# A two-layer hybrid encoder on one core: a hand-written planner with new instruction costs, two buffers for the recurrence's keys and decays, and a key move without a chain

## The chip, the cores and the metric

The kernel runs on one core of a Trainium2 chip. The metric is the device time of one execution in microseconds (us); it was 1365.31 us as the median of three runs (1364.5 to 1365.95). One more execution was profiled; the trace below is of that one.

## The reference

The input is one sequence of 512 tokens with 1024 channels in float32. Two layers are computed. Cut to what matters:

```python
for l in range(2):
    sh1, sc1, g1, sh2, sc2, g2 = split(silu(c) @ w_ada[l] + b_ada[l], 6)
    h = rmsnorm(x, norm1_w[l]) * (1 + sc1) + sh1
    proj = h @ w_in[l]            # 3584 columns, split among three mixers
    a   = silu(layernorm(depthwise_conv31(a_val * sigmoid(a_gate))))   # 256 channels
    att = mixture of three dilated windows, ALiBi, 6 heads of 64       # 384 channels
    rec = HGRN2 in both directions, 6 heads of 64, gated by silu(g)    # 384 channels
    x = x + g1 * (concat(a, att, rec) @ w_out[l])
    h = rmsnorm(x, norm2_w[l]) * (1 + sc2) + sh2
    u = depthwise_conv3(h @ w_up[l])
    x = x + g2 * ((gelu(u[:, :2816]) * u[:, 2816:]) @ w_down[l])
return rmsnorm(x, final_norm_w)
```

The recurrence's gates are `f = lb + (1 - lb) * sigmoid(z)`, and its keys `(1 - lb) * sigmoid(-z)`, one pair for each direction.

## The kernel before, in words

**Layout.** Channels lie on the 128 partitions and the 512 tokens along the free dimension. The residual stream is eight tiles `x0` to `x7`. A projection works in output tiles of 128 channels: a weight chunk of 128x1024 float32 is loaded into a raw buffer (`wr`), split into a high and a low part of a shorter float type (`wh`, `wl`), and three products (high by high, high by low, low by high) are summed in one PSUM bank. So an input projection tile is 8 x 3 = 24 matmuls of 512 columns, an output projection tile of four inputs is 12. PSUM has two banks for the main stream of tiles (`g`), four for the mixers (`m`) and one double bank (`m2`).

**Stages of a layer.** (1) The first six projection tiles run together, chunk by chunk, as the modulated input appears (`first_group`). (2) In the mixer stretch the other 22 input tiles follow one at a time, in the order of `REST`, then eight output projection tiles over four of the eight mixed tiles; between them run the three mixers: the convolution of 31 taps (VectorE, 31 steps for each of two channel tiles), the attention (for each of three pairs of heads eight score tiles, each: two matmuls, exponentials, a reciprocal, four transposes) and the recurrence (for each of three pairs of heads seven levels of 32 small matmuls with VectorE products on `KK`, the decayed keys, `QQ`, the queries, and `TT`, the gates). (3) The rest of the output projection and the norm's sums close the mixers (`last_group`). (4) The MLP: 44 tiles up, 22 down, and a second `last_group`.

**What sets the order.** Nothing is reordered by a compiler. Each piece of work is a Python generator, a thread with a priority (`spawn`), that yields what it needs next: tiles that must be written, buffers, a float such as `DM`, `CM`. `run_threads` keeps a model of the engines (`Clock`): every instruction that is issued advances its engine by a cost from a formula, and the thread of the best priority that is ready by TensorE's modelled time goes next. So the cost formulas and priorities decide in which order the instructions stand in each engine's queue; on the chip every engine then works its own queue in that order and waits on semaphores. Among the priorities are those of the recurrence `RP` = 1.0, the attention `AP` = 2.0 and the convolution `CP` = 2.5 (a smaller number goes first); the main stream has 9. Loads and moves inside the chip's memory are all issued by SyncE (SP), in the planner's order as well.

**The parts that the change touches.** `BUFFERS` lists for each kind of tile its size in KB a partition and its count: five raw weight buffers `wr`, one `KK`, one `TT`. In `evac`, the branch for a gate tile (`Z_F`) takes a `KK` and a `TT` buffer; `rec` gives them back near its end. `mm` and `transpose` hold TensorE's cost formulas. `shift` issues a move of 64 partitions to the other 64, and books its end at 2.4 us after the transfer.

**The key move.** The scores of a head pair come from one query tile and two key tiles, `t[0]` for the first head and `t[1]` for the second; each holds the high part of a head's keys in that head's half of the partitions and the low part in the other half. The key branch copies the PSUM tile once into `t[0]` (high), subtracts (low), and then issues three moves: two from `t[0]` into the halves of `t[1]`, and one inside `t[0]` from half to half, which overwrites what one of the first two reads:

```python
for hd in range(2):
    self.shift(t[1][own[hd]], t[0][own[1]])
self.shift(t[0][own[1]], t[0][own[0]])
```

Of the kernel before, what the change touches and what calls it, by code (L numbers as in the profile page):

```python
# [9 lines left out]
F32 = mybir.dt.float32  # L10
F32R = mybir.dt.float32r
# [27 lines left out]
H2 = T // 2  # L39


BUFFERS = dict(wr=(4, 5), wh=(4, 4), wl=(4, 4), hx=(4, 8), qk=(4, 3), PT=(4, 4), KK=(4, 1), QQ=(4, 1), S=(4, 1),
               TT=(6, 1), ao=(2, 2), vr=(2, 2), va=(2, 1), bias=(4, 2), wa=(4, 1), tmp=(2, 5), P=(2, 2), sc=(1, 1),
               ap=(4.25, 1), acc=(2, 2), sm=(0.03125, 8), km=(2, 1), gs=(2, 3), qr=(2, 2), t2=(2, 2))
ORDER = ["wh", "wl", "wa", "bias", "wr", "tmp", "km", "P", "ap", "acc", "gs", "qr", "vr", "va", "ao", "t2", "sc",
         "hx", "PT", "TT", "qk", "KK", "QQ", "S", "sm"]
# [34 lines left out]
ADAF = 0.2  # L81
WAR = 0.1
CM = 1.0
CP = 2.5
FINE = 1
WA = 5
SM = 0.2
# [11 lines left out]
ADAP = 1.0  # L99
ADAM = 2.0  # L100
BIAS = 0.8


NPE = 5
# [88 lines left out]
class Kernel:  # L193
    def __init__(self, ctx, tc, a):
# [13 lines left out]
        self.free_slots, self.slot, self.count = {}, {}, 0  # L208
        for tag, (kb, n) in BUFFERS.items():
            self.free_slots[tag] = [dict(tag=tag, name=f"{tag}{i}", size=int(kb * 256), pool=self.one, last=0.0)  # L210
# [62 lines left out]
    def shift(self, out, in_):  # L273

        self.nc.sync.dma_start(out=out.bitcast(F32), in_=in_.bitcast(F32))
        c = self.clk
        t = max(c.t.get("DMA", 0.0), c.t["PE"], c.written(in_) or 0.0) + size(in_) * in_.shape[0] * 4 / 350e3
        c.t["DMA"] = t
        lo, hi = span(out)
        c.w.setdefault(out.tensor.name, []).append((lo, hi, t + 2.4, "DMA"))  # L280
        c.last[out.tensor.name] = t + 2.4

    def mm(self, out, lhsT, rhs, start, stop, **kw):
        self.nc.tensor.matmul(out, lhsT=lhsT, rhs=rhs, start=start, stop=stop, **kw)  # L284
        n, m = size(out), out.shape[0]
        c = 0.009 + n * 0.000408 if rhs.dtype == F32R else n * 0.00168 * {32: 0.5, 64: 0.51}.get(m, 1.0)
        self.clk.issue("PE", c, [out], [lhsT, rhs])

    def transpose(self, out, in_):
        self.nc.tensor.transpose(out, in_, self.ident)  # L290
        self.clk.issue("PE", 0.109, [out], [in_])


    def spawn(self, gen, prio, slack=0.0):
# [235 lines left out]
                                        ALU.add, ALU.mult)  # L530

    critical = False

    def ada_thread(self, l, order, tags, margin, every=0.0):
        order, w, t0 = list(order), [], 0.0
# [367 lines left out]
    def evac(self, l, n, ps):  # L903

        cur, v, sc = self.cur, self.v, self.s
# [9 lines left out]
        elif n >= I_REC:  # L915
            p = n - I_REC
            yield (ps, "tmp")
            t = self.sb([128, T], "tmp")
            self.copy(t, ps)
            self.give(ps)  # L920
            cur["V", p] = self.spawn(self.to_tokens(t, "vr"), 0, SLACK)
        elif n >= Z_F:
            d, p = (0, n - Z_F) if n < Z_B else (1, n - Z_B)
            yield (ps, "tmp") + (("KK", "TT") if d == 0 else (lambda: 0.0 if ("KK", p) in cur else None,))
            s = self.sb([128, T], "tmp")
            if d == 0:
                cur["KK", p] = self.sb([128, 2, T], "KK")
                cur["TT", p] = self.sb([128, 3, T], "TT")
            KK, TT = cur["KK", p], cur["TT", p]
            sc.activation(s, ps, AF.Sigmoid)  # L930
            sc.activation(KK[:, d], ps, AF.Sigmoid, scale=-1.0)
            self.give(ps)
            j = 3 * d + p
            lb, oml, tml = (self.lb[:, i, l, j:j + 1] for i in range(3))
            yield (s, DM)
            v.tensor_scalar(s, s, oml, tml, ALU.mult, ALU.max)
            yield (s, DM)
            self.shifted(TT[:, d], s, lb)
            if d == 0:
                self.shifted(TT[:, 2], s, lb)  # L940
            self.give(s)
            yield (KK[:, d], DM)
            self.scaled(KK[:, d], KK[:, d], oml)
            if d:
                cur["zb", p] = True
        elif n >= V_ATT:
            p = n - V_ATT
            yield (ps, "tmp")
            t = self.sb([128, T], "tmp")
            self.copy(t, ps)  # L950
            self.give(ps)
            cur["Va", p] = self.spawn(self.to_tokens(t, "va"), 0, SLACK)
            yield (lambda: 0.0 if ("qa", p) in cur and ("ka", p) in cur else None,)
            self.spawn(self.att(l, p), AP, SLACK)
        elif n >= Q_ATT:
            q = n < K_ATT
            p = n - Q_ATT if q else n - K_ATT
            own = [slice(0, 64), slice(64, 128)]
            if q:

                yield (ps, "qk", "tmp")
                t = self.sb([128, 2, T], "qk", F32R)
                lo = self.sb([128, T], "tmp", F32R)
                sc.activation(t, ps.unsqueeze(1).to_broadcast([128, 2, T]), AF.Copy, scale=-0.125)
                yield (t[:, 0], DM)
                v.scalar_tensor_tensor(lo, ps, -0.125, t[:, 0].bitcast(F32), ALU.mult, ALU.subtract)
                self.give(ps)
                yield (lo,)
                for hd in range(2):
                    self.shift(t[own[1 - hd], hd], lo[own[hd]])  # L970
                self.give(lo)
            else:

                yield (ps, ["qk", 2])
                t = [self.sb([128, 2, T], "qk", F32R) for _ in range(2)]
                self.copy(t[0][:, 0], ps)
                yield (t[0][:, 0], DM)
                v.tensor_tensor(out=t[0][:, 1], in0=ps, in1=t[0][:, 0].bitcast(F32), op=ALU.subtract)
                self.give(ps)
                yield (t[0],)  # L980
                for hd in range(2):
                    self.shift(t[1][own[hd]], t[0][own[1]])
                self.shift(t[0][own[1]], t[0][own[0]])
            cur["qa" if q else "ka", p] = t
        elif n >= A_GATE:
            yield (ps, "acc")
            s = self.sb([128, T], "acc")
            sc.activation(s, ps, AF.Sigmoid)
            self.give(ps)
            cur["ag", n - A_GATE] = s  # L990
        else:
            if n == 0:
                yield ("ap",)
                cur["apad"] = self.sb([128, 2, T + CW - 1], "ap")
                self.gp.memset(cur["apad"][:, :, :CW // 2], 0.0)
                self.gp.memset(cur["apad"][:, :, T + CW // 2:], 0.0)
            yield (ps, lambda: 0.0 if ("ag", n) in cur and "apad" in cur else None)
            yield (cur["ag", n], DM)
            v.tensor_tensor(out=cur["apad"][:, n, CW // 2:CW // 2 + T], in0=ps, in1=cur["ag", n], op=ALU.mult)
            self.give(ps)  # L1000
            self.th["conv", n] = self.spawn(self.conv(l, n), CP, SLACK)
        for p in range(3):
# [466 lines left out]
```

## Time and profile before

| what | value |
|---|---|
| median of the timed runs | 1365.31 us |
| the profiled execution's own time | 1367.1 us |
| its span, first to last instruction | 1365.3 us |
| TensorE busy | 97% of the span |
| VectorE busy | 78% |
| ScalarE busy | 45% |
| mean granted TensorE clock | 0.992 |

The profile is one execution taken by the hardware profiler. PE is TensorE's matmul, PEld its weight load, DVE is VectorE, ACT ScalarE, SP SyncE. The busy share of PE counts the time between a matmul's start and its modelled end, so that waits show as idle stretches between them. The views used below are: the windows (busy time of every engine between two times, with the granted clock `PEclk`, 1.00 being full speed), the waits (who waited for whom: us in total, times, longest), the timeline (instructions in order of time, with the idle time before them in brackets), the chain of work that ended last (start, us, what), the groups by shape (busy us, mean ns), and the DMA issues (KB each, median us to landing). All arithmetic goes through a few helpers, so their lines (L181, L284, L290, in `Engine`, `mm` and `transpose`) name nothing; the tile names do.

### The profile page before, as it was taken

The page shows a single profiled execution, that of the slowest core. Times are in us where ns is not written, and L with a number is a line of the kernel's source. Part 1 is how long each engine was busy: PE and PEld are TensorE (multiplying, and loading weights), DVE is VectorE, ACT ScalarE, POOL GpSimd, SP SyncE. Part 2 cuts the span into 40 slices and gives each one's busy share as a digit, 9 for nine tenths or more (in the row PEclk, how much of TensorE's full clock was granted, in tenths as well). Part 3 has the DMA queues.
Part 4 walks back from the last instruction along what each step waited for, and adds up shares of the span by engine and source line. Part 5 has one row for each costly group of instructions (what it writes and reads, how often), then busy time and mean ns, then how long its engine had stood idle before and what let it go on. Part 6 is the DMA issues. An engine that isn't in the chain of part 4 may idle for free.

```text
span 1365.3 us, 24377 instructions
## 1 busy us (share of the span) xinstructions
PE 1328.6 (97%) x9936; PEld 1103.7 (81%) x9936; DVE 1060.7 (78%) x1820; ACT 611.2 (45%) x1024; POOL 2.1 (0%) x16
## 2 busy tenths in 40 slices
PE   8998999999999999999999999999899999999997
PEld 7976777779988888888898786777798888888887
DVE  6898889987698999666785998888667565666666
ACT  5535548574442333233453473758445232333332
POOL 0000000000000000000000000000000000000000
PEclk9999999999999999999999999999999999999998
DMA  9645353342358787421612413114221423233221
GB/s 360 214 147 160 121 170 109 106 122 96 122 157 318 221 289 250 140 100 47 193 49 80 133 62 112 34 48 145 92 76 48 139 64 107 85 105 119 62 78 63
DMA packets 57664, 175.48 MB, mean 129 GB/s; under 512 B 6736, under 2 KB 8784, under 8 KB 57552
## 3 DMA queue, kind: packets, MB, share of 16 engines
q1 hardware_dynamic: 57552, 173.92, 39.7%
q8 instruction: 78, 1.28, 0.4%
q14 instruction: 34, 0.28, 0.1%
HBM read 165.50 MB, written 2.10 MB: 123 GB/s over the span
## 4 chain that ended last, share of the span: by engine, by line
PE 79%; DVE 13%; DMA 4%; ACT 2%; issue 2%; SPq 0%; DVEq 0%; ACTq 0%
PE m L284 52%; PE g L284 25%; DVE acc L181 2%; DMA qk<-qk 2%; DVE wl L181 2%; PE m L290 2%; DVE QQ L181 1%; DVE KK L181 1%; DVE P L181 1%; DVE tmp L181 1%; DVE TT L181 1%; DVE wa L181 1%; ACT P L181 1%; DVE x L181 1%; ACT wh L181 0%
## 5 line engine op out<-in xcount | busy, mean ns | idle before, releaser
L284 PE MATMUL g<-hx,wh 128*128 128x512 f32 (+1 forms) x1280 | 402.7, 391 | 0.5 <-DVE qr L181 0.3
L284 PE MATMUL m<-hx,wh 128*128 128x512 f32 (+1 forms) x1152 | 324.4, 365 | 1.1 <-DVE hx L181 1.1
L284 PEld LDWEIGHTS g<-hx,wh 128*128 128x128 f32 x1280 | 235.4, 189 | 49.2 <-issue 3.9
L181 DVE TENSOR_TENSOR wl<-wr,wh 128x1024 fp32r<-128x1024 f32 (+3 forms) x212 | 217.5, 1028 | 69.7 <-ACT wh L181 63.8
L181 ACT CAST wh<-wr 128x1024 fp32r<-128x1024 f32 (+3 forms) x174 | 154.8, 891 | 236.4 <-PE m L284 161.6
L284 PE MATMUL g<-hx,wl 128*128 128x512 f32 (+1 forms) x636 | 248.1, 390 | 0.0
L284 PEld LDWEIGHTS m<-hx,wh 128*128 128x128 f32 x1152 | 207.7, 189 | 36.5 <-DVE hx L181 1.7
L284 PE MATMUL m<-hx,wl 128*128 128x512 f32 (+1 forms) x584 | 211.2, 362 | 0.0
L284 PEld LDWEIGHTS g<-hx,wl 128*128 128x128 f32 x636 | 119.9, 188 | 22.6 <-issue 0.2
L284 PEld LDWEIGHTS m<-hx,wl 128*128 128x128 f32 x584 | 110.2, 189 | 16.8
L181 DVE SCALAR_TENSOR_TENSOR x<-m,mod,x 128x256 f32<-128x256 f32 (+1 forms) x112 | 66.3, 593 | 43.0 <-PE m L284 42.4
L181 DVE SCALAR_TENSOR_TENSOR acc<-ap,par,acc 128x512 f32<-128x512 f32 x120 | 89.7, 747 | 2.1
L181 DVE SCALAR_TENSOR_TENSOR tmp<-m,par,tmp 128x511 f32<-128x511 f32 x120 | 89.3, 747 | 2.0
L181 ACT ACTIVATE P<-P,sm 128x512 f32<-128x512 f32 x78 | 56.2, 723 | 49.5 <-DVE sm L181 49.3
L181 DVE CAST wh<-wr 128x1024 fp32r<-128x1024 f32 (+3 forms) x42 | 25.3, 603 | 51.8 <-PE m L284 38.3
L181 ACT ACT_TABLE_LOAD x49 | 62.9, 1283 | 4.9 <-DVE tmp L181 3.3
L181 ACT ACTIVATE tmp<-tmp 128x512 f32<-128x512 f32 x44 | 27.8, 633 | 77.2 <-DVE tmp L181 77.2
L181 ACT COPY km<-KK 128x512 f32<-128x512 f32 x30 | 20.6, 685 | 82.5 <-DVE KK L181 59.2
L181 DVE CUSTOM_DVE_ANT_0 wa<-wa,cb,par 128x1024 f32<-128x1024 f32 x40 | 51.1, 1279 | 7.1 <-DMA wa<-w_ada 7.0
L181 ACT ACTIVATE tmp<-m,par 128x512 f32<-128x512 f32 x60 | 40.6, 685 | 31.1 <-PE m L284 28.9
L181 DVE CUSTOM_DVE_ANT_0 bias<-bias,cb,par 128x1024 f32<-128x1024 f32 x39 | 49.6, 1279 | 1.6 <-DMA bias<-w_ada 1.6
L181 DVE SCALAR_TENSOR_TENSOR tmp<-g,par,tmp 128x511 f32<-128x511 f32 x56 | 41.8, 747 | 10.5 <-ACT tmp L181 9.5
(310 smaller groups left out, 2097.5 us busy)
## 6 DMA issues: line engine op xcount, KB each, us to landing
wr<-w_up SPq DMA_DIRECT2D x76, 512.0 KB, 3.5
wr<-w_in SPq DMA_DIRECT2D x44, 512.0 KB, 3.9
wa<-w_ada SPq DMA_DIRECT2D x40, 512.0 KB, 3.9
bias<-w_ada SPq DMA_DIRECT2D x39, 512.0 KB, 4.5
wr<-w_down SPq DMA_DIRECT2D x32, 320.0 KB, 3.0
wr<-w_down SPq DMA_DIRECT2D x32, 256.0 KB, 2.6
wr<-w_in SPq DMA_DIRECT2D x16, 384.0 KB, 5.7
wr<-w_up SPq DMA_DIRECT2D x16, 384.0 KB, 3.1
```

The lines of the kernel that those rows point to most:

```text
L181: r = f(*a, **k)
L284: self.nc.tensor.matmul(out, lhsT=lhsT, rhs=rhs, start=start, stop=stop, **kw)
L290: self.nc.tensor.transpose(out, in_, self.ident)
```

## The change

It has five parts.

1. The planner's TensorE costs: a 512-column product is booked at 0.0135 + 512 x 0.000417 us, the small ones of the recurrence at 0.016 us where they stood at 0.027, and 0.1 us is added wherever the shape of the array that a matmul uses differs from that of the one before (`SWITCH`). These are numbers of the planner; the instructions are the same.
2. A move inside the chip's memory is booked at 4.5 us after the transfer instead of 2.4, it replaces older entries of the same range, and its source counts as in use until then.
3. `KK` and `TT` have two buffers; `wr` has three instead of five.
4. `CP` is 1.5, so that the convolution stands ahead of the attention.
5. The key branch copies the PSUM tile into both key tiles, subtracts into `t[0]`, copies the low part into `t[1]`, and issues one move in each key tile, from one half to the other. The copies are fixed to ScalarE.

```diff
-BUFFERS = dict(wr=(4, 5), wh=(4, 4), wl=(4, 4), hx=(4, 8), qk=(4, 3), PT=(4, 4), KK=(4, 1), QQ=(4, 1), S=(4, 1),
-               TT=(6, 1), ao=(2, 2), vr=(2, 2), va=(2, 1), bias=(4, 2), wa=(4, 1), tmp=(2, 5), P=(2, 2), sc=(1, 1),
+BUFFERS = dict(wr=(4, 3), wh=(4, 4), wl=(4, 4), hx=(4, 8), qk=(4, 3), PT=(4, 4), KK=(4, 2), QQ=(4, 1), S=(4, 1),
+               TT=(6, 2), ao=(2, 2), vr=(2, 2), va=(2, 1), bias=(4, 2), wa=(4, 1), tmp=(2, 5), P=(2, 2), sc=(1, 1),
...
-CP = 2.5
+CP = 1.5
...
+SWITCH = 0.1
...
     def shift(self, out, in_):
...
-        c.w.setdefault(out.tensor.name, []).append((lo, hi, t + 2.4, "DMA"))
-        c.last[out.tensor.name] = t + 2.4
+        l = c.w.setdefault(out.tensor.name, [])
+        l[:] = [e for e in l if not (lo <= e[0] and e[1] <= hi)] + [(lo, hi, t + 4.5, "DMA")]
+        c.last[out.tensor.name] = c.last[in_.tensor.name] = t + 4.5
...
     def mm(self, out, lhsT, rhs, start, stop, **kw):
...
-        c = 0.009 + n * 0.000408 if rhs.dtype == F32R else n * 0.00168 * {32: 0.5, 64: 0.51}.get(m, 1.0)
-        self.clk.issue("PE", c, [out], [lhsT, rhs])
+        mode = (lhsT.shape[0], m)
+        if rhs.dtype == F32R:
+            c = 0.0135 + n * 0.000417
+        elif mode == (128, 128):
+            c = max(0.17, n * 0.00168 + 0.005)
+        else:
+            c = {(64, 32): 0.016, (128, 32): 0.027}.get(mode, n * 0.00086)
+        self.clk.issue("PE", c + (SWITCH if mode != self.mode else 0.0), [out], [lhsT, rhs])
+        self.mode = mode
...
                 t = [self.sb([128, 2, T], "qk", F32R) for _ in range(2)]
-                self.copy(t[0][:, 0], ps)
+                for hd in range(2):
+                    self.s.copy(t[hd][:, 0], ps)
                 yield (t[0][:, 0], DM)
                 v.tensor_tensor(out=t[0][:, 1], in0=ps, in1=t[0][:, 0].bitcast(F32), op=ALU.subtract)
                 self.give(ps)
-                yield (t[0],)
+                yield (t[0][:, 1],)
+                self.s.copy(t[1][:, 1], t[0][:, 1].bitcast(F32))
+                yield (t[1],)
                 for hd in range(2):
-                    self.shift(t[1][own[hd]], t[0][own[1]])
-                self.shift(t[0][own[1]], t[0][own[0]])
+                    self.shift(t[hd][own[1 - hd]], t[hd][own[hd]])
```

**What it moves.** In all, TensorE has the same 8013 matmuls in another order, VectorE 1815 instructions where it had 1822, ScalarE 999 for 978 (two more table loads among them, 51 for 49), and SP 409 for 415. The array's shape changes 155 times along TensorE's queue in both orders.

SP's queue in layer 0 around the keys of the second head pair (`qk` the query and key tiles, `wr` raw weights, `wa` modulation weights, `bias` the attention's distance terms), before:

```order
L275 DMA qk_296_1981<-tmp_297_1982 64x512 x2
L263 DMA wa_304_2077<-w_sh 128x1024
L263 DMA wr_315_2162<-w_in 128x1024
L275 DMA qk_309_2101<-qk_308_2100 64x1024 x2
L275 DMA qk_308_2100<-qk_308_2100 64x1024
L263 DMA wa_316_2184<-w_ada 128x1024
L263 DMA bias_322_2239<-bias 128x896
L263 DMA bias_323_2240<-bias 128x896
```

and now:

```order
L276 DMA qk_292_1959<-tmp_293_1960 64x512 x2
L264 DMA wa_300_2019<-w_sh 128x1024
L264 DMA wa_307_2137<-w_ada 128x1024
L264 DMA wr_314_2168<-w_in 128x1024
L276 DMA qk_309_2143<-qk_309_2143 64x1024
L276 DMA qk_310_2144<-qk_310_2144 64x1024
L264 DMA bias_320_2233<-bias 128x896
L264 DMA bias_321_2234<-bias 128x896
```

Three moves, the third of which reads and writes what the first two read, have become two that touch different tiles; the bias loads still stand behind them.

TensorE's queue at the first scores of that pair (`g` tiles are the main stream, `m<-qk,qk` the scores, `m<-QQ,km` a level of the recurrence), before; the last matmul of the key tile stands 34 main-stream matmuls ahead of the first scores:

```order
L284 MATMUL m_0_317_2186<-QQ_290_1966,km_314_2159 32x32 x32
L284 MATMUL g_307_2098<-hx_17_200,wh_274_1865 128x512 x2
L284 MATMUL g_307_2098<-hx_17_200,wl_278_1878 128x512
L284 MATMUL g_307_2098<-hx_18_201,wh_274_1865 128x512 x2
L284 MATMUL g_307_2098<-hx_18_201,wl_278_1878 128x512
...
L284 MATMUL g_320_2235<-hx_13_196,wl_288_1956 128x512
L284 MATMUL g_320_2235<-hx_14_197,wh_285_1934 128x512
L284 MATMUL m_328_2257<-qk_308_2100,qk_296_1981 128x512 x2
```

and now, 45 main-stream matmuls ahead:

```order
L286 MATMUL m_0_327_2257<-QQ_286_1944,km_316_2225 32x32 x32
L286 MATMUL g_318_2229<-hx_15_198,wh_277_1886 128x512
L286 MATMUL g_318_2229<-hx_15_198,wl_282_1916 128x512
L286 MATMUL g_318_2229<-hx_16_199,wh_277_1886 128x512
L299 MATMUL m_329_2295<-ident,tmp_319_2231 128x128 x4
...
L286 MATMUL g_318_2229<-hx_17_200,wh_277_1886 128x512 x2
L286 MATMUL g_318_2229<-hx_17_200,wl_282_1916 128x512
L286 MATMUL m_333_2315<-qk_309_2143,qk_292_1959 128x512 x2
```

The scores have moved back by 11 matmuls and by one more level of the recurrence. For the six head pairs of the two layers the count is 30, 34, 24, 44, 42, 31 before and 54, 45, 26, 42, 48, 27 now.

ScalarE's queue at the end of layer 1's mixers (`P` the attention's probabilities, `sm` small columns, here the recurrence's norm, whose square root needs another function table than the exponential), before:

```order
L181 ACTIVATE P_1579_10062,sm_1581_10064<-P_1579_10062,sm_1580_10063 128x512
L181 ACT_TABLE_LOAD
L181 ACTIVATE sm_1574_10048<-sm_1574_10048,eps 128x8
...
L181 ACTIVATE P_1579_10062<-P_1579_10062,sm_1581_10064 128x512
L181 ACT_TABLE_LOAD
L181 ACTIVATE P_1588_10098,sm_1590_10100<-P_1588_10098,sm_1589_10099 128x512
L181 CAST wh_1594_10123<-wr_1569_10031 128x768
```

and now:

```order
L182 ACTIVATE P_1559_9997,sm_1561_9999<-P_1559_9997,sm_1560_9998 128x512
L182 COPY PT_1497_9726<-m_1554_9981 128x2x128
L182 ACT_TABLE_LOAD
L182 ACTIVATE sm_1557_9995<-sm_1557_9995,eps 128x8
L182 ACT_TABLE_LOAD
L182 ACTIVATE P_1563_10015,sm_1565_10017<-P_1563_10015,sm_1564_10016 128x512
L182 CAST wa_1571_10046<-wr_1539_9907 128x1024
L182 ACTIVATE P_1572_10048,sm_1574_10050<-P_1572_10048,sm_1573_10049 128x512
```

The square root's two table loads stood between the last two score tiles' exponentials; now they stand one tile earlier, and the last tile's exponential follows with no load between.

More of the change, by code (lines that the diff above doesn't have):

```diff
@@ L285, in mm @@
         n, m = size(out), out.shape[0]
-        c = 0.009 + n * 0.000408 if rhs.dtype == F32R else n * 0.00168 * {32: 0.5, 64: 0.51}.get(m, 1.0)
-        self.clk.issue("PE", c, [out], [lhsT, rhs])
+        mode = (lhsT.shape[0], m)
[7 more added lines that the diff above has]
+        self.mode = mode
     def transpose(self, out, in_):
         self.nc.tensor.transpose(out, in_, self.ident)
-        self.clk.issue("PE", 0.109, [out], [in_])
+        self.clk.issue("PE", 0.109 + (SWITCH if self.mode != (128, 128) else 0.0), [out], [in_])
+        self.mode = (128, 128)
     def spawn(self, gen, prio, slack=0.0):
@@ L532 @@
     critical = False
+    mode = (128, 128)
     def ada_thread(self, l, order, tags, margin, every=0.0):
```

## The prediction, made before the changed kernel had been run

> **What bounds the kernel now.** First the page's head and its row of engines.
>
> ```profile
> span 1365.3 us, 24377 instructions
> PE 1328.6 (97%) x9936; PEld 1103.7 (81%) x9936; DVE 1060.7 (78%) x1820; ACT 611.2 (45%) x1024; POOL 2.1 (0%) x16
> ```
>
> TensorE is busy in 1328.6 of 1365.3 us, and the change removes no matmul. All an order can bring lies in TensorE's 36.7 us of idle time and in stretches at a lower clock. Second, the windows by stage (start, mixers and feed-forward of layer 0, the same of layer 1); the columns are length, busy time of TensorE, its loads, VectorE, ScalarE and GpSimd, granted clock, DMA share, GB/s.
>
> ```profile
> 0.00:66.00 66.00, 61.15 (x506) 56.41 (x507) 48.26 (x108) 32.98 (x66) 1.95 (x14) 1.00 0.81 297
> 66.00:307.00 241.00, 229.89 (x2651) 175.90 (x2652) 219.33 (x422) 141.85 (x259) 0.00 (x0) 0.98 0.43 132
> 307.00:736.00 429.00, 427.53 (x2238) 367.25 (x2235) 338.56 (x532) 166.31 (x257) 0.18 (x2) 1.00 0.49 163
> 736.00:966.00 230.00, 219.87 (x2565) 170.93 (x2565) 200.61 (x384) 134.52 (x237) 0.00 (x0) 0.99 0.30 87
> 966.00:1357.00 391.00, 388.99 (x1984) 332.75 (x1979) 250.43 (x368) 135.58 (x208) 0.00 (x0) 1.00 0.28 85
> ```
>
> The feed-forwards (third and fifth row) leave 1.5 and 2.0 us idle: nothing to gain. The mixers leave 241.00 − 229.89 = 11.1 and 230.00 − 219.87 = 10.1, together **21.2 us**, and only there is the clock under 1.00. VectorE is busy there 219.33/241 = 91% and 200.61/230 = 87%, ScalarE 59% and 58%. So TensorE bounds the mixers, VectorE stands close behind it, and the waits are those of single tiles that come too late. Third, who ends TensorE's waits (total, times, longest).
>
> ```profile
> PE m L284 <- DMA qk<-qk: 6.0, 5, 2.0
> PE m L290 <- ACT P L181: 3.9, 3, 3.4
> PE m L290 <- DVE P L181: 3.4, 2, 2.0
> ...
> PE g L284 <- DVE qr L181: 0.3, 1, 0.3
> ```
>
> The key moves cost 6.0 us, the probabilities P ahead of their transposes 3.9 + 3.4 = 7.3. These are 13.3 of the mixers' 21.2; the other 21.2 − 13.3 = 7.9 are spread over small waits. Fourth, the clock, in windows cut around the waits (the eighth figure is the granted clock).
>
> ```profile
> 128.00:132.00 4.00, 2.02 (x15) 1.59 (x14) 3.93 (x10) 2.63 (x6) 0.00 (x0) 0.98 0.31 121
> 132.00:138.70 6.70, 6.70 (x28) 6.26 (x29) 4.28 (x11) 5.74 (x9) 0.00 (x0) 0.50 0.46 147
> ...
> 187.00:189.90 2.90, 0.85 (x4) 0.67 (x4) 0.94 (x2) 1.09 (x2) 0.00 (x0) 1.00 0.93 258
> 189.90:193.30 3.40, 3.40 (x73) 2.59 (x72) 2.67 (x4) 0.00 (x0) 0.00 (x0) 0.50 0.92 310
> 958.00:961.30 3.30, 0.16 (x1) 0.00 (x0) 2.41 (x5) 1.36 (x3) 0.00 (x0) 1.00 0.41 119
> 961.30:964.70 3.40, 3.13 (x9) 1.98 (x11) 0.95 (x2) 1.37 (x4) 0.00 (x0) 0.50 0.38 120
> ```
>
> Three stretches, 6.7 + 3.4 + 3.4 = 13.5 us, ran at 0.50, each right behind a wait. At half the clock half the work is done, so they lost about 13.5 × 0.5 = 6.75 us, counted as busy time.
>
> **The key moves.** The keys of the second head pair of layer 0, from the chain of waits (start, length) and the timeline (start, length, in brackets the idle time before and its releaser):
>
> ```profile
> 180.59 5.42 DMA qk<-qk
> 186.07 2.93 DMA qk<-qk
> ```
> ```profile
> 189.05 1.37 PE L284 MATMUL m<-qk,qk 128*128 128x512 f32 x4 [2.05 <-DMA qk<-qk]
> ```
>
> The third move waits for the first two (5.42 us) and takes 2.93 more, and TensorE stands idle for 2.05. The change drops that hop of 2.93 and puts one more ScalarE copy of the low half ahead of the moves. The copy's size is that of the query tile's cast (ScalarE, count, busy, mean ns):
>
> ```profile
> L181 ACT CAST qk<-tmp 128x512 fp32r<-128x512 f32 x12 | 7.4, 619 | 29.4 <-DVE tmp L181 29.4
> ```
>
> So the keys come 2.93 − 0.62 = 2.3 us sooner, more than the longest of the five waits, 2.05. The orders add to it: behind the key tile stood 34 main-stream matmuls ahead of the first scores in this pair, now 45. Of the six pairs the cover falls in two, from 44 to 42 and from 31 to 27; 4 matmuls are about 0.9 us by the rate quoted below, under 2.3. I take the whole row: **−6.0**. Bounds: 0, if the copies queue behind ScalarE's work, and −6.0. The two extra copies for each of six head pairs are 12 × 0.62 = 7.4 us of ScalarE, hidden in its idle 99 and 95 us of the mixers; uncovered, they would cost 0.62 each ahead of a move, 3.7 for six. On SP's queue two transfers replace three, and the bias loads behind them wait for one hop less.
>
> **The P waits.** The timeline, at the two places where they cost most:
>
> ```profile
> 127.81 0.63 PE L290 MATMUL m<-ident,P 128*128 128x128 f32 x4 [1.37 <-DVE P L181]
> 130.88 0.66 PE L290 MATMUL m<-ident,P 128*128 128x128 f32 x4 [1.98 <-DVE P L181]
> ```
> ```profile
> 955.76 1.28 ACT L181 ACT_TABLE_LOAD   x1
> 957.05 0.72 ACT L181 ACTIVATE P<-P,sm 128x512 f32<-128x512 f32 x1
> ...
> 960.79 0.72 ACT L181 ACTIVATE P<-P,sm 128x512 f32<-128x512 f32 x1 [1.94 <-DVE sm L181]
> 961.57 1.11 PE L290 MATMUL m<-ident,P 128*128 128x128 f32 x4 [3.41 <-ACT P L181]
> ```
>
> At 961.57 the last tile of layer 1 is late: its exponential at 957.05 stood behind a table load of 1.28, and the scaling at 960.79 came 0.78 ahead of the transposes. In the new order the two loads stand one tile earlier, and 31 main-stream matmuls lie between scores and transposes where there were 21. A main-stream matmul is 27.20/120 = 0.227 us:
>
> ```profile
> 446.47 27.20 PE m L284 x120
> ```
>
> So 10 × 0.227 = 2.3 of cover and 1.28 of load: 3.5 us against a wait of 3.41, which goes. In layer 0 the two late tiles had 8 and 9 matmuls of cover, the least of all; the new order's least is 11. Two or three matmuls are 0.45 to 0.7, so by cover alone the two waits of 1.37 and 1.98 would shrink, not go. But the tiles around them have moved too; of these two I take the larger away and leave 1.37. Term: −(3.41 + 1.98) = **−5.4**; bounds 0 and −7.3.
>
> **The slow clock.** The stretches lost 6.75 us and each follows one of the waits above. If these go, so do they, but a new wait may start one: of 3.4 us, 1.7 lost. I take −6.75 + 1.7 = **−5.0**; bounds 0 and −6.75. As the rows have it, idle times of 1.98 and 2.05 us were enough for a stretch at 0.50. The Trainium skill, page "TensorE: Matmul & The Clock Gate", section "What's actually happening", says that the gate throttles after an idle window of about 3.4 us; by that only the last of the three stretches would be due to an idle time, and the traces disagree with it at the other two.
>
> **What the new order brings of its own.** The 7.9 us of small waits stay in number, as far as the diff tells: nothing in it makes their tiles faster. But all instructions were laid anew, and VectorE, at 91% and 87%, now has the convolution's steps ahead of attention's. What these and the added table loads (51 where there were 49) take:
>
> ```profile
> L181 DVE SCALAR_TENSOR_TENSOR acc<-ap,par,acc 128x512 f32<-128x512 f32 x120 | 89.7, 747 | 2.1
> ```
> ```profile
> L181 ACT ACT_TABLE_LOAD x49 | 62.9, 1283 | 4.9 <-DVE tmp L181 3.3 <-PEq L1460 0.7
> ```
>
> An attention tile on VectorE that finds two or three convolution steps ahead of it is 1.5 to 2.2 us late, as much as the waits of now. So new waits between 0 and another 7.9 (as many small ones as stand there today); I take **+5**, nearer the upper end, as VectorE has so little room. A gain here isn't in the trace's rows beyond the other terms, except that the 7.9 could go too.
>
> **KK and TT double**, and the planner's shape-change price: the nearest row in which TensorE's main stream waits for the recurrence is qr's 0.3 us, and the array's shape changes 155 times in both orders. **0**, bounds −0.3 and 0. The raw weight buffers, five to three, pay for the space; that is a rival below, and in the sum 0.
>
> **Sum**: −6.0 − 5.4 − 5.0 + 5 = −11.4 against the profiled run's own 1367.1 gives 1355.7. That run is 1.8 above the median of 1365.31, so the median forecast is 1355.7 − 1.8 = 1353.9, **1354**. By the bounds of the terms: all at their best, 1365.3 − 6.0 − 7.3 − 6.75 = 1345; the own range of this case, with most of the moves' and P's gain and new waits from 0 to 8, is 1348 to 1358.
>
> **Rivals.** *Everything goes*: the small waits too, as the planner's durations now fit the trace. 21.2 + 6.75 = 28 us are there; about nine tenths of it gives 1340. For it: the costs of before booked the moves at 2.4 us where the trace has 5.42. Against it: VectorE's 91%. Chance 0.12.
>
> *The waits only move*: VectorE delivers as late as before, wherever the order puts the wait; the moves' 6.0 turn into waits for P or the convolution's tiles, and so does the clock's loss. Time 1365, no change. For it: the same 219 and 201 us of VectorE work in 241 and 230 us. Against it: the waits of now sit at few places with little cover. Chance 0.16.
>
> *The slow stretches aren't the waits' doing*: two of the three have waits of about 2 us ahead of them, but also tens of narrow matmuls (73 in the stretch at 189.90), and low activity of this kind stays whatever the order. Then the third term is −1.7 at most: 1365.3 − 6.0 − 5.4 − 1.7 + 5 = 1357.2, or 1359 without it. The Trainium skill's rule named above would give the same. Chance 0.10.
>
> *Slower: three raw weight buffers run dry*. What SP waits for, and what a slot's round of 256 KB consists of (SP's issue, least and median ns; landing from issue, the last figure, us; cast on ScalarE; subtraction on VectorE):
>
> ```profile
> SPq L263 <- DVE wl L181: 722.1, 190, 18.9
> SPq L263 <- DVE mod L181: 115.3, 49, 11.1
> ```
> ```profile
> L263 SPq DMA_DIRECT2D wr<-w_out x24: 327/328/563, 193.1 to 939.9; - x24
> ```
> ```profile
> wr<-w_out SPq DMA_DIRECT2D x16, 256.0 KB, 2.7
> ```
> ```profile
> L181 ACT CAST wh<-wr 128x512 fp32r<-128x512 f32 x37 | 23.0, 621 | 45.7 <-PE g L284 24.6 <-PE m L284 21.1
> ```
> ```profile
> L181 DVE TENSOR_TENSOR wl<-wr,wh 128x512 fp32r<-128x512 f32 x48 | 32.9, 686 | 10.0 <-ACT wh L181 8.3 <-PE g L284 1.0
> ```
>
> A round is 0.33 + 2.7 + 0.62 + 0.69 = 4.3 us, plus any time W that SP waits for something else ahead of the load. Three slots give a chunk every (4.3 + W)/3 us; TensorE uses one in 12 × 0.227 = 2.72. Four split buffers hold 4 × 2.72 = 10.9 us, and a group has 8 chunks, so they run dry once 8 × ((4.3 + W)/3 − 2.72) is over 10.9, from W = 8.0. At W = 9 it is 8 × 1.71 − 10.9 = 2.8 us a group; two groups of output weights and four of layer 0's down projection make 17 us: 1354 + 17 = 1371. With five slots it would be 13.3/5 = 2.66, under 2.72, never dry. For it: a longest wait of 11.1 in the second row. Against it: that row's mean is 115.3/49 = 2.4. Chance 0.18.
>
> **How the numbers follow.** The forecast has the rest, 1 − 0.12 − 0.16 − 0.10 − 0.18 = 0.44. A measurement of this kernel can tell about 0.2%, or 2.7 us, from no change. Faster are the forecast, the first and the third rival, 0.44 + 0.12 + 0.10 = 0.66; the same 0.16; slower 0.18. The range reaches from 1339, which takes in the best rival, to 1369, which takes in the second and the smaller part of the last; outside are most of the last rival, about 0.14, and some 0.05 below.
>
> **What would show it right or wrong.** Right: no key-move wait on TensorE, no 3.41 at the end of layer 1's mixers, at most one window at 0.50, and the mixers' idle near 21.2 − 6.0 − 5.4 + 5 = 14.8. The first rival: that idle under 5. The second: 20 or more, with VectorE's tiles as releasers. The third: windows at 0.50 without a wait ahead. The last: TensorE or ScalarE waiting for the weights' transfers, in the feed-forwards too. Wrong altogether: a change of the busy time of TensorE by over 10 us at full clock, since the matmuls are the same.

## The result and the profile after

The changed kernel took 1352.86 us (median of four runs, 1352.18 to 1353.67), the kernel before 1365.53: ratio 0.9909, 95% interval 0.9896 to 0.9922, some 12.4 us less (12.7 by the medians). The forecast was 1354. The profiled run took 1353.67 with a span of 1351.9, 13.4 less than before's. First the head and the row of engines of the changed kernel's page.

```profile
span 1351.9 us, 24362 instructions
PE 1325.4 (98%) x9936; PEld 1102.8 (82%) x9936; DVE 1056.5 (78%) x1813; ACT 626.1 (46%) x1045; POOL 2.1 (0%) x16
```

The same 9936 matmul records; TensorE's idle time is 1351.9 − 1325.4 = 26.5 us where it was 36.7, and its busy time is 3.2 us less. So there are two sources: 10.2 us of waits and about 3 of clock. Where the idle time went is seen in the windows of the two mixers, cut in both kernels at nearly the same work, from the stretch's start to the first matmuls of its last output projection. (The first mixer really begins at 63.16 before and at 67.04 after; no idle time lies between these and the cut at 66.) Before:

```profile
66.00:312.44 246.44, 234.58 (x2673) 178.21 (x2672) 221.47 (x425) 143.83 (x264) 0.00 (x0) 0.98 0.42 130
736.00:968.96 232.96, 222.49 (x2577) 172.27 (x2575) 201.35 (x386) 135.87 (x239) 0.00 (x0) 0.99 0.29 86
```

And after:

```profile
66.00:307.00 241.00, 233.98 (x2696) 180.68 (x2695) 221.71 (x425) 156.83 (x282) 0.00 (x0) 0.99 0.42 133
729.70:955.32 225.62, 221.52 (x2573) 169.71 (x2572) 199.72 (x381) 139.38 (x246) 0.00 (x0) 1.00 0.27 83
```

Layer 0's idle time falls from 11.9 to 7.0, layer 1's from 10.5 to 4.1: 11.2 us. VectorE does the same work (221.5 and 221.7, 201.4 and 199.7 us) in less time. Who ends TensorE's waits in the changed kernel (total, times, longest):

```profile
PE g L286 <- DVE TT L182: 3.2, 1, 3.2
PE m L286 <- DVE tmp L182: 2.5, 2, 1.4
PE m L286 <- ACT tmp L182: 2.2, 1, 2.2
PE g L286 <- DVE gs L182: 1.9, 2, 1.0
PE m L286 <- ACT km L182: 1.9, 2, 1.5
PE m L299 <- ACT P L182: 1.2, 2, 1.0
PE m L286 <- DVE sm L182: 1.1, 1, 1.1
```

The row of 3.2 at the top is the kernel's first matmul, and stood there before too. No row names the key moves any more (6.0 before). P has 1.2 us where it had 7.3. New is a wait of 2.2 us for the recurrence's transposed tile `tmp`; here it is in the timeline, with the transposes and with VectorE's and ScalarE's rows.

```profile
201.44 0.82 PE L299 MATMUL m<-ident,KK 128*128 128x128 f32 x6
...
202.01 1.22 DVE L182 TENSOR_TENSOR wl<-wr,wh 128x1024 fp32r<-128x1024 f32 x1
...
202.91 1.03 ACT L182 CAST wh<-wr 128x1024 fp32r<-128x1024 f32 x1
203.15 0.55 DVE L182 COPY tmp<-m 128x384 f32<-128x384 f32 x1
...
203.96 0.48 ACT L182 COPY tmp<-m 128x384 f32<-128x384 f32 x1
...
204.49 0.57 PE L286 MATMUL m<-vr,tmp 128*64 128x64 f32 x12 [2.24 <-ACT tmp L182]
```

The transposes behind `tmp` were done at about 202.3. Both copies of the result then stood behind one piece of weight preparation each, 1.22 us on VectorE and 1.03 on ScalarE. That wait is followed by the only half-clock stretch of the changed kernel's mixers (the granted clock is the third figure from the right):

```profile
203.24:206.65 3.41, 1.88 (x20) 1.26 (x20) 3.34 (x8) 3.36 (x5) 0.00 (x0) 1.00 0.64 172
206.65:213.48 6.83, 5.93 (x27) 4.13 (x28) 5.08 (x14) 4.06 (x8) 0.00 (x0) 0.50 0.41 116
```

### The profile page after: what moved, and what is told of

It reads as the page before. It is cut to its first block, busy times and chain, and to the rows that moved or that the text cites. A ratio compares the mean times of both kernels' runs of the same rounds, so it can differ in the third digit from the quotient of the medians.

```text
span 1351.9 us, 24362 instructions
## 1 busy us (share of the span) xinstructions
PE 1325.4 (98%) x9936; PEld 1102.8 (82%) x9936; DVE 1056.5 (78%) x1813; ACT 626.1 (46%) x1045; POOL 2.1 (0%) x16
## 3 DMA queue, kind: packets, MB, share of 16 engines
q8 instruction: 78, 1.28, 0.4%
## 4 chain that ended last, share of the span: by engine, by line
PE 88%; DVE 8%; ACT 2%; issue 1%; DMA 0%; SPq 0%; DVEq 0%; ACTq 0%
PE m L286 54%; PE g L286 32%; PE m L299 2%; DVE acc L182 1%; DVE P L182 1%; DVE wl L182 1%; DVE QQ L182 1%; DVE x L182 1%; DVE KK L182 1%; DVE PT L182 1%; ACT P L182 1%; DMA x<-xT 0%; DVE tmp L182 0%; DVE gs L182 0%; DVE TT L182 0%
## 5 line engine op out<-in xcount | busy, mean ns | idle before, releaser
L286 PE MATMUL m<-hx,wh 128*128 128x512 f32 (+1 forms) x1096 | 315.2, 371 | 1.0 <-ACT hx L182 0.7
L286 PE MATMUL g<-hx,wl 128*128 128x512 f32 (+1 forms) x644 | 251.1, 390 | 0.0
L286 PEld LDWEIGHTS m<-hx,wh 128*128 128x128 f32 x1096 | 200.0, 189 | 36.7 <-ACT hx L182 0.9
L286 PE MATMUL m<-hx,wl 128*128 128x512 f32 (+1 forms) x568 | 207.9, 366 | 0.0
L286 PEld LDWEIGHTS m<-hx,wl 128*128 128x128 f32 x568 | 107.7, 190 | 17.1
L182 DVE SCALAR_TENSOR_TENSOR x<-m,mod,x 128x256 f32<-128x256 f32 (+1 forms) x112 | 66.2, 591 | 41.9 <-PE m L286 41.4
L182 ACT ACTIVATE P<-P,sm 128x512 f32<-128x512 f32 x73 | 52.4, 722 | 38.6 <-DVE sm L182 38.0
L182 ACT ACTIVATE tmp<-x 128x256 f32<-128x256 f32 (+1 forms) x64 | 28.4, 444 | 45.3 <-DVE x L182 39.6
```

The lines of the kernel that those rows point to most:

```text
L182: r = f(*a, **k)
```

## The experiments

There are twelve. The first two keep the order of TensorE and VectorE instruction by instruction and change the key moves alone; the others, up to the eleventh, let the planner lay its order anew, as the change itself does. The last one is about the clock. Differences between runs are taken from the ratios to the kernel before that was timed beside them.

**1. The key moves alone, in the old order.** The planner is told of the old copies and moves, and the new ones are issued (`shift` with `False` books a move and issues none):

```diff
                 self.copy(t[0][:, 0], ps)
+                self.nc.scalar.copy(t[1][:, 0], ps)
...
+                self.nc.scalar.copy(t[1][:, 1], t[0][:, 1].bitcast(F32))
                 for hd in range(2):
-                    self.shift(t[1][own[hd]], t[0][own[1]])
-                self.shift(t[0][own[1]], t[0][own[0]])
+                    self.nc.sync.dma_start(out=t[hd][own[1 - hd]].bitcast(F32), in_=t[hd][own[hd]].bitcast(F32))
+                    self.shift(t[1][own[hd]], t[0][own[1]], False)
+                self.shift(t[0][own[1]], t[0][own[0]], False)
```

> The kernel before with the two independent key moves in place of the three chained ones, and nothing else: TensorE, VectorE and the loads keep their order of before, instruction by instruction (ScalarE has two more copies per head pair, SP one move less). Theory A, the chain itself cost the waits for the keys: the row of 6.0 us goes, and with it the stretch at half clock behind the wait at 189 (1.7 us lost), so the time falls by 5.5 to 7.7 us, to 1358 to 1360. Rival B, the waits only move to the next late tile, since VectorE delivers as late as before: the row goes but other waits come, and the time falls by less than 2 us, to 1363.5 or more.

Ratio 0.9956, interval 0.994 to 0.9972: 6.0 us less (3.8 to 8.2; the medians, 1360.69 for 1365.96, give 5.3). No key-move wait is left, and the place behind the scores of the second head pair, at half clock in the kernel before, has the full clock:

```profile
185.60:189.00 3.40, 3.40 (x77) 2.65 (x76) 2.31 (x5) 2.05 (x3) 0.00 (x0) 1.00 0.91 325
189.00:192.40 3.40, 3.40 (x19) 2.69 (x16) 2.98 (x5) 0.00 (x0) 0.00 (x0) 1.00 0.36 107
```

The waits that have nothing to do with the keys stay:

```profile
PE m L291 <- ACT P L181: 3.9, 3, 3.4
PE m L285 <- DVE sc L181: 3.5, 6, 1.1
PE m L291 <- DVE P L181: 3.3, 2, 2.0
...
PE m L291 <- DVE KK L181: 1.9, 1, 1.9
```

Some did move. In the kernel before, the two rows were

```profile
PE m L284 <- DVE sc L181: 2.6, 5, 1.1
PE m L290 <- DVE KK L181: 1.2, 1, 1.2
```

The wait for KK is 1.9 for 1.2, just behind the first pair's scores, whose wait of 0.61 is gone; a new one of 0.87 for `sc` stands at 193.55, just behind the place where TensorE had been at half clock. So the 6.0 us of time are not the 6.0 us of the row alone: the row went, the stretch at half clock went with it (1.7 lost), and about 1.6 us of other waits came in their place. Theory A holds, and this is the one term whose cause is shown by itself.

**2. The old chain in the new order.** The reverse: the changed kernel, its planner told of the new copies and moves, issues the old three moves, without the two added copies (the diff shows the moves).

```diff
-                for hd in range(2):
-                    self.shift(t[hd][own[1 - hd]], t[hd][own[hd]])
+                for hd in range(2):
+                    self.nc.sync.dma_start(out=t[1][own[hd]].bitcast(F32), in_=t[0][own[1]].bitcast(F32))
+                self.nc.sync.dma_start(out=t[0][own[1]].bitcast(F32), in_=t[0][own[0]].bitcast(F32))
+                for hd in range(2):
+                    self.shift(t[hd][own[1 - hd]], t[hd][own[hd]], False)
```

> The changed kernel with the old three chained key moves, and nothing else: TensorE, VectorE and the loads keep the new order. In the changed kernel's trace the first scores stand 7.85, 6.0, 7.0, 6.55, 5.67 and 6.08 us behind the issue of the second move; in the trace of before the key tile was ready some 8.7, 8.5, 7.1, 8.15, 6.85 and 6.6 us behind it. The old code has no copy of the low half ahead of the moves, so it issues them 2.5, 0.65, 1.1, 1.1, 2.5 and 0.65 us sooner. What is left over is 1.85 in the second pair and 0.5 in the fourth. Theory A, chain and cover both count: 2 to 4 us more than the changed kernel's 1352.9, so 1355 to 1357. Rival B, the order alone did it: no more than 1 us, 1352 to 1354. Rival C, the chain alone, whatever the order: 6 to 7.7 us more, 1359 to 1360.5.

1357.94, ratio 0.9934 (0.9922 to 0.9947): 3.4 us more than the changed kernel by the ratios (0.9934 − 0.9909, of 1366), inside theory A's 2 to 4, and 5.1 by the medians, just over it. Only part of it shows as a wait for the keys; another came as a P wait that the changed kernel hasn't:

```profile
PE m L304 <- DVE P L182: 1.3, 1, 1.3
...
PE m L291 <- DMA qk<-qk: 0.8, 2, 0.6
```

The P wait is the chain's doing as well, by way of SP's queue. The third move waits there for the first two, and the loads behind it wait with it. In the first pair, the changed kernel's `wa` load first, then this run's rows:

```profile
115.24 0.33 SPq L264 DMA_DIRECT2D wa<-w_ada  x1
```
```profile
114.58 0.46 SPq L1003 DMA_DIRECT2D qk<-qk  x1
116.92 0.38 SPq L264 DMA_DIRECT2D wa<-w_ada  x1
124.63 1.28 DVE L182 CUSTOM_DVE_ANT_0 wa<-wa,cb,par 128x1024 f32<-128x1024 f32 x1 [3.06 <-DMA wa<-w_ada]
128.03 0.66 PE L304 MATMUL m<-ident,P 128*128 128x128 f32 x4 [1.28 <-DVE P L182]
```

The load goes out 1.7 us later, close behind three others. VectorE, which has no wait for it in the changed kernel, stands idle until it lands, and the attention's P, which comes behind it in VectorE's queue, is late for TensorE. All six third moves together held SP's queue for 23.7 us (24.0 in the kernel before). The half-clock stretches of the mixers come to the same here, 3.41 twice for 6.83 once.

So the key moves are worth 6 us in the old order and 3 to 5 in the new one, whose cover hides a part of the chain. Rivals B and C fall.

**3. The new prices alone.** The kernel before with the changed kernel's `mm` and `transpose` costs and `SWITCH = 0.1`.

> The kernel before with the planner's new prices for matmuls and for a change of the array's shape, and nothing else: old key moves, one KK and one TT, convolution behind attention, moves booked at 2.4. Theory A, the matmul prices are what lays the probabilities' transposes far enough behind: the waits for P fall from 7.3 to under 2.5 and the half-clock stretches behind them go, while the key moves' 6.0 stays: 5 to 10 us less, 1355.5 to 1360.5. Rival B, the prices alone give another order of the same quality: within 3 us of 1365.5.

Ratio 0.9995 (0.9983 to 1.0008): no gain. P's waits do fall, from 7.3 to 3.8, but others come in their place, and 10.2 us of the mixers still run at half clock:

```profile
PE m L285 <- DMA qk<-qk: 5.6, 5, 2.3
PE m L285 <- ACT st L182: 3.3, 2, 1.9
...
PE m L298 <- ACT P L182: 2.3, 3, 1.9
...
PE m L298 <- DVE P L182: 1.5, 2, 0.8
```

Theory A had the mechanism half right and the time wrong; rival B holds.

**4 to 6. One part taken out of the changed kernel.** `CP = 2.5`; one KK and one TT with five raw buffers; the old matmul prices, without `SWITCH` (of each diff the main line).

```diff
-CP = 1.5
+CP = 2.5
```
```diff
-wr=(4, 3) ... KK=(4, 2) ... TT=(6, 2)
+wr=(4, 5) ... KK=(4, 1) ... TT=(6, 1)
```
```diff
-        c = 0.0135 + n * 0.000417
+        c = 0.009 + n * 0.000408
```

> The changed kernel with the convolution's priority back at 2.5, behind attention, and nothing else; the planner lays a quarter of TensorE's rows elsewhere. Theory A, the convolution ahead is what keeps attention's last tiles covered: the wait of 3.41 us for the last P of layer 1 and its half-clock stretch (1.7 lost) come back in some form, 3 to 6 us more than 1352.9, so 1356 to 1359. Rival B, the priority is of no weight: 1350 to 1356. Rival C, any re-laying of an order that was picked for its time costs much, as the nudge of before did (16 us): over 1360.

> The changed kernel with one KK and one TT and five raw weight buffers as before, and nothing else; over half of TensorE's rows stand elsewhere. Theory A (the prediction's), the doubling hides nothing and three raw buffers cost nothing: 1350 to 1356. Rival B, the double tiles let a pair of the recurrence start beside the one before, and that is the gain beyond the moves: 5 to 8 us more, 1358 to 1361, with TensorE waiting for KK or TT. Rival C, re-laying costs, over 1361, without such waits.

> The changed kernel with the planner's old prices of matmuls and none for a change of shape, and nothing else (moves still booked at 4.5). Theory A, the prices alone give nothing, as in the kernel before (ratio 0.9995): 1350 to 1356. Rival B, they count only together with the free key moves and the double tiles: 5 us more or over, 1358 to 1362, with waits for P and half-clock stretches back. Rival C, re-laying costs, over 1362.

- *Convolution behind attention*: ratio 0.9923 (0.9903 to 0.9942), about 2 us more than the changed kernel, which these intervals don't tell from nothing; by its time rival B holds. Theory A's mechanism shows in small: layer 1's last two P tiles are late by 0.4 and 1.5 us, without a half-clock stretch. The larger new wait, 4.8 us for the output projection's activations in layer 0, with 6.8 us at half clock behind it, is none of the theories'.
- *One KK and TT*: 0.9933 (0.9916 to 0.995), about 3 us more, just over theory A's upper end, again with overlapping intervals. TensorE waits for KK once in the mixers, for 0.1 us, and for TT never, so rival B's waits weren't there; what came are waits for P (6.6 us) and 17.1 us at half clock, in a profiled execution that was some 5 us slower than the other three.
- *Old prices*: 0.9944 (0.9929 to 0.9959), 4.8 us more, clear of the changed kernel, in the gap between its theory A and its rival B. The waits are for the recurrence's `sc` (5.4 us) and for a weight load on its way to layer 0's modulation (5.0); P has 2.3 for 1.2. Rival B's half-clock stretches did come back: 17.1 us in the mixers for 6.8.

**7 to 10. A nudge that means nothing.** The planner's margin behind a result, 0.5 to 0.6 in the kernel before (7) and in the changed one (8), and to 0.4 in both (9 and 10).

```diff
-SLACK = 0.5
+SLACK = 0.6
```

> The kernel before with one margin of the planner, by which a thread waits behind a result, at 0.6 instead of 0.5: it says nothing new of the chip, but lays a quarter of TensorE's rows elsewhere. Theory A, an order is good by the durations it is laid from: the time stays within 3 us of 1365.5, as the waits move about. Rival B, a good part of what an order brings is chance: the time moves by 3 us or more, either way.

> The changed kernel with the margin behind a result at 0.6 instead of 0.5, the same nudge that cost the kernel before 16 us. Theory A, the time of a laid order is to a good part chance, and both settings are ones that came out well: 3 to 17 us more than 1352.9, 1356 to 1370. Rival B, durations nearer to the trace make the order robust: within 3 us, 1350 to 1356.

> The kernel before with the margin behind a result at 0.4 instead of 0.5, the nudge to the other side. Theory A, the old prices make a fragile order, whose time is chance: 5 us or more over 1365.5. Rival B, the 16 us of the first nudge were one bad case: within 3 us.

> The changed kernel with the margin at 0.4 instead of 0.5. Theory A, the new prices and free moves make the order robust, as the first nudge showed (ratio 0.992 for 0.9909): 1350 to 1357. Rival B, that was one good case: over 1360.

| kernel | margin 0.4 | 0.5 | 0.6 |
|---|---|---|---|
| before | 0.9986 (0.9973 to 0.9998) | 1 | 1.0118 (1.0103 to 1.0133) |
| changed | 0.9981 (0.9972 to 0.9991) | 0.9909 (0.9896 to 0.9922) | 0.9920 (0.9898 to 0.9943) |

So one nudge cost the kernel before 16 us and the other gave it 2; of the changed kernel the first cost 1.5, which isn't told from nothing, and the second 10. The view that the new prices make the order robust, which the first pair of runs bore out, fell with the second pair. Where the 16 us went is worth a look:

```profile
span 1382.0 us, 24362 instructions
...
PE 1340.6 (97%) x9936; PEld 1113.1 (81%) x9936; DVE 1058.0 (77%) x1808; ACT 606.8 (44%) x1031; POOL 2.1 (0%) x16
```
```profile
PE m L284 <- DMA qk<-qk: 10.8, 4, 2.9
PE m L290 <- DVE P L181: 6.8, 4, 2.4
```
```profile
128.50:142.15 13.65, 9.92 (x41) 8.54 (x42) 12.74 (x34) 8.91 (x18) 0.00 (x0) 0.50 0.34 115
```

Idle time grew by 4.7 us (41.4 for 36.7), but busy time by 12.0, with the same matmuls: 44.4 us of the mixers ran at half clock where it had been 13.7, one stretch of 13.65 alone, with P waits of 2.43, 1.04 and 1.28 us around its start and in it. So 4.7 us more of idle time came with a span 16.7 us longer; the rest is clock.

**11. Three raw weight buffers alone**, in the kernel before.

```diff
-wr=(4, 5)
+wr=(4, 3)
```

> The kernel before with three raw weight buffers instead of five, and nothing else (a tenth of TensorE's rows stand elsewhere). Theory A (the prediction's forecast), three are enough: within 3 us of 1365.5. Rival B (the prediction's slower case), they run dry behind SP's longest waits: up to 17 us more, to 1382, with TensorE waiting for split weights in the feed-forward.

Ratio 0.9982 (0.997 to 0.9994): 2.5 us less, not more, and TensorE has no wait for split weights. The raw buffers do run short, for ScalarE: its waits for their loads, most of them in the feed-forwards, are 26.3 us here and 32.8 in the changed kernel, where the kernel before had 0.2. The largest rows, before and in the changed kernel:

```profile
ACT wh L181 <- DMA wr<-w_in: 0.2, 1, 0.2
```
```profile
ACT wh L182 <- DMA wr<-w_up: 18.6, 7, 3.8
ACT wh L182 <- DMA wr<-w_down: 4.1, 1, 4.1
```

TensorE didn't feel it: in layer 0's feed-forward (307.00 to 729.70 in the changed kernel) it was busy for all of the 422.70 us. The rival that ended slower falls.

One more thing is seen here. The wait of 3.41 us for layer 1's last P, the largest of before in the mixers, is 0.06 in this order (0.81 for the tile ahead of it). In the other three orders laid anew from the kernel before (experiments 3, 7 and 9) it is 0.68, nothing and nothing. So each of these orders was nearly rid of it, the one that took 16 us more as well.

**12. The clock by itself.** Idle times of chosen length among the feed-forward's full-width matmuls, where nothing else waits:

```diff
+        nc.tensor.matmul(ps[:, :1], lhsT=self.spare, rhs=self.mean32, start=True, stop=True)
+        for _ in range(n):
+            nc.gpsimd.memset(self.spare, 0.0)
+        nc.tensor.matmul(ps[:, :1], lhsT=self.spare, rhs=self.mean32, start=True, stop=True)
```

> The changed kernel with idle times put into the two feed-forward networks, where TensorE otherwise runs flat out on full-width matmuls: every 14 us or so a one-column matmul reads a spare tile, GpSimd overwrites that tile 2 to 17 times (0.2 us each in the trace of before), and another one-column matmul waits for it, so that TensorE stands idle for about 0.9 to 4 us, eight lengths in turn, some five times each. Theory A (the prediction's), an idle time of 2 us is enough: stretches at 0.50 behind nearly all stalls of 2 us and more, none behind those under 1.3. Rival B, only an idle time of 3.4 us is enough: half-clock stretches behind the one longest length alone. Rival C, the narrow matmuls of the mixers count as well, and an idle time among full-width matmuls has to be longer than the mixers' 2 us: no stretch behind stalls of 2 to 2.5 us, though they started one in the mixers. The time itself says nothing (some 40 stalls, 80 to 120 us longer).

The run took 1531.91 us with 40 stalls. How many of each length had a stretch at 0.50 right behind:

| idle, us | 0.58 to 0.91 | 1.43 to 1.62 | 1.96 to 2.15 | 2.74 to 2.94 | 3.27 to 3.46 | 3.79 to 4.78 |
|---|---|---|---|---|---|---|
| at half clock behind | 0 of 10 | 3 of 5 | 4 of 5 | 4 of 5 | 4 of 5 | 10 of 10 |

Theory A holds: two microseconds are mostly enough, and even 1.43 can be. Rivals B and C fall. What decides between equal lengths is where the idle time falls. Two stalls in the timeline, one of 1.43 and one of 3.27 us:

```profile
558.28 0.38 PE L749 MATMUL m<-mean,spare 128*128 128x1 f32 x2 [1.43 <-POOL spare L748]
```
```profile
618.73 0.38 PE L749 MATMUL m<-mean,spare 128*128 128x1 f32 x2 [3.27 <-POOL spare L748]
```

Windows of 3.41 us, cut so that each half-clock stretch of this run begins at an edge:

```profile
555.71:559.12 3.41, 1.98 (x12) 1.64 (x11) 3.06 (x6) 1.63 (x2) 1.02 (x5) 1.00 0.72 251
559.12:562.53 3.41, 3.41 (x10) 2.65 (x9) 3.37 (x6) 0.41 (x1) 0.00 (x0) 0.50 0.65 223
...
613.67:617.09 3.42, 1.79 (x10) 1.43 (x8) 1.95 (x3) 1.04 (x1) 1.22 (x6) 1.00 0.59 222
617.09:620.50 3.41, 1.77 (x9) 1.52 (x10) 0.35 (x1) 0.00 (x0) 1.24 (x7) 1.00 0.44 154
620.50:623.91 3.41, 3.41 (x17) 2.83 (x16) 1.81 (x2) 1.06 (x1) 0.00 (x0) 1.00 0.02 5
```

The 1.43 us lie within one window (3.41 − 1.98) and the next is at half clock. The 3.27 us are split by an edge into 1.6 and 1.6, and no window behind is slow. Sorted over all windows of that run behind 300 us that were at full clock themselves: with up to 1.41 us idle none is followed by a slow one, from 1.42 to 1.68 four of nine, from 1.83 all 22.

## Why the prediction was right, point by point

The time was right to 1.1 us, and a part of that is luck: two terms held about in size, two were off by 1.6 and 3.1 in opposite directions, and one of those that held did so by a wrong step. For the profiled runs:

| term | forecast | measured | how |
|---|---|---|---|
| key moves | −6.0 | −6.0 | the row of 6.0 is gone |
| P waits | −5.4 | −6.1 | 7.3 to 1.2 |
| slow clock | −5.0 | −3.4 | 13.7 to 6.8 us at half clock in the mixers, half of it lost |
| new waits | +5 | +1.9 | idle time without keys and P: 36.7 − 13.3 = 23.4, now 26.5 − 1.2 = 25.3 |
| sum | −11.4 | −13.6 | span −13.4 |

- **Key moves.** Size and mechanism right, and shown (experiment 1): the row goes in the old order too. The gain in time there, 6.0 (3.8 to 8.2), is smaller than the row and its half-clock stretch together, 6.0 + 1.7, as other waits took up 1.6. The price hangs on the order: in the new one the chain would cost 3 to 5 (experiment 2), in part through SP's queue, which the prediction names for the bias loads and gives no price.
- **P waits.** Near in size, but not by the steps given. The count of cover was misread: along TensorE's queue, between scores and transposes, the two late tiles of layer 0 had 42 and 5 main-stream matmuls, not 8 and 9. And cover doesn't tell which tile is late: in the changed kernel tiles with 9 to 12 aren't late by more than 0.03, and the one that is late by 1.04, in layer 1, has 38. The 1.37 that was left in layer 0 is gone as well. The wait of 3.41 at layer 1's end went, as forecast; but it also went in every new order of the kernel before (experiment 11), so the moved table loads are not shown to be the cause. Nor are the prices: alone they brought P's 7.3 to 3.8 and no time.
- **Slow clock.** The sign was right and one stretch did come back, but of 6.8 us, not 3.4: that term was mis-sized by 1.6. "Each follows one of the waits" holds for the stretches of before, as a rule of all kernels it is too narrow (below).
- **New waits.** Mis-sized by 3: the mixers have only 0.9 more of other waits (22.3 − 13.3 = 9.0, now 11.1 − 1.2 = 9.9) and the start 1.8 (4.9 to 6.7), a stage that the sum left out; the rest of the kernel has 0.8 less. The mixers' idle time is 11.1 us, where about 15 was named as a sign. The mechanism named, a tile of attention or recurrence behind other work on VectorE, is what the 2.24 us at 204.49 shows, except that weight preparation stood ahead and not the convolution.
- **KK and TT, shape price, raw buffers at 0.** The wait of 1.2 us for KK that the mixers of before had, a row that the prediction passes over, is gone. But with the new prices alone it is gone as well, and with one KK and TT only 0.1 us for KK is left (experiments 3 and 5), so the second buffer isn't needed to remove it. The shape price wasn't tested apart from the matmul prices. Three raw buffers alone didn't cost anything (experiment 11).
- **Rivals.** That everything goes: no, 11.1 us of idle time are left in the mixers. That the waits only move: not for the keys; for the prices alone it is just what happened. The slow stretches as not the waits' doing: refuted as the main cause by experiments 1 and 12. Slower by raw buffers: refuted in time, though its sign appeared, ScalarE waiting for the weights' transfers; the split buffers hid it from TensorE.

What stays open is the rest of the gain, 12.4 − 6.0 = 6.4 us by the ratios. It comes from the order as it was laid, and the waits that went can be named. But which part of the change made it isn't settled: taking the prices out costs 4.8, putting them in gives nothing, the new booking of the moves (4.5 us for 2.4) was never taken out by itself, and a margin moved by 0.1, which stands for nothing on the chip, moves either kernel by between −2 and +16 us. So 6.4 us are within what any re-laying does, and a story for each part would be one told after the fact.

## What to carry to other kernels

Where a planner lays the order, test a part of a change with the order held (book the old step, issue the new one); only then is a difference that part's own. Before crediting prices or priorities with a gain, nudge a number that means nothing and see how far the time moves: here by as much as the gain. Look at what a slow transfer holds up in its queue, and not only at who waits for its data: the third key move also delayed the loads behind it. And count more than its length for a wait of TensorE of about 2 us: behind the 1.98 at 130.88 in the kernel before came 6.83 us at half clock, some 3.4 lost.

## What the runs showed of the hardware

The half-clock stretches of one run start on one grid. In the kernel before they start at 131.88, 189.90, 961.31 and 1357.26 us: 58.02, 771.41 and 395.95 apart, which is 17, 226 and 116 times 3.413.

```profile
131.88:138.71 6.83, 6.83 (x29) 6.38 (x29) 4.40 (x11) 5.86 (x9) 0.00 (x0) 0.50 0.45 145
189.90:193.31 3.41, 3.41 (x73) 2.60 (x72) 2.68 (x4) 0.00 (x0) 0.00 (x0) 0.50 0.92 309
961.31:964.72 3.41, 3.15 (x9) 1.98 (x11) 0.94 (x2) 1.36 (x4) 0.00 (x0) 0.50 0.38 120
```

From run to run the grid lies elsewhere against the work. The same wait of 2.2 us starts a stretch of 6.8 us in one kernel (206.65 in the changed one) and of 3.4 in another with the same order (210.87 in experiment 2); that the grid makes this difference is likely, and not shown. Within a window it took about 1.4 to 1.8 us of idle time, near half of it, not a window without work (experiment 12). The Trainium skill, page "TensorE: Matmul & The Clock Gate", section "What's actually happening", gives the window as 3413 ns and free-running; the traces agree with both. It also has the clock fall after at least one idle window; here windows that were busy for 1.98 of 3.41 us were enough.

Idle time isn't all that counts. In experiment 2 a stretch began behind a window in which TensorE was busy throughout, with 85 matmuls, 64 of them on 64 rows and 32 columns of the array and 16 more with a single column of data:

```profile
258.66:262.07 3.41, 3.41 (x85) 3.22 (x84) 1.72 (x7) 0.95 (x3) 0.00 (x0) 1.00 0.58 153
262.07:265.48 3.41, 3.41 (x13) 2.75 (x11) 2.46 (x6) 1.49 (x3) 0.00 (x0) 0.50 0.73 275
```

Two more kernels have such a stretch behind a window without idle time and with many narrow matmuls, at 254.50 (experiment 5) and at 261.62 (experiment 7). So the prediction's third rival had a small part of the truth. What share of the array a window has to keep busy wasn't measured.
